# RWKV bonus kept in the mix, a finer planner clock, and another order of the input projections, in a hybrid recurrent layer

## The chip, the cores and the metric

The kernel runs on one core of one Trainium2 chip. The metric is the device time of one execution in microseconds; the median of three runs before is 1594.51 us (1593.97 to 1595.9).

## The reference

One inference step of one layer, all in float32: a prompt of 1024 tokens with zero states, and 8 sample tokens with states of their own (1032 columns together), model width 1024.

```
xn = rmsnorm(x);  P = xn @ w_in            # 1024 x 3456 columns
pr, ph, pl = split(P)                      # RWKV-7 (6 heads), HGRN2 (6 heads), RG-LRU (256 channels)
# A) RWKV-7: pm = pr + mu * (shift(pr) - pr); r, k, v, lora inputs; per token and head
S = S * w_t + (S @ -kk_t) (kk_t * a_t)^T + v_t k_t^T ;   out_t = S r_t
gn    = groupnorm(out) * ln_w + ln_b
bonus = (sum(r * k * r_k) * v)             # per head
o_r   = (gn + bonus) * g
# B) HGRN2: S = f_t * S + (1 - f_t) i_t^T ; o_t = S^T q_t ; rmsnorm per head, silu gate
# C) RG-LRU: conv of width 4, two gates, h_t = a_t h_{t-1} + sqrt(1 - a_t^2) (i_t x_t), gelu gate
mix = concat(o_r, o_h, o_l)                # 384 + 384 + 256
x = x + mix @ w_out
x = x + square(relu(rmsnorm(x) @ mlp_w1)) @ mlp_w2      # 1024 -> 4096 -> 1024
y = rmsnorm(x)
```

Returned are y for both groups and the five final states of each.

## The kernel before

Activations lie transposed, features on the partitions: mix is eight tiles of 128 features, three for RWKV (a pair of heads each), three for HGRN, two for LRU. Time is cut into two halves: half 0 is tokens 0 to 511, half 1 tokens 512 to 1023 with the 8 samples (520 columns). A dense product is done in three reduced-precision (fp32r) matmuls for each block of 128 features: weights and activations are split into a high and a low part (wh, wl, xh, xl, for the output projection mh, ml), and wh x xh, wh x xl, wl x xh are summed. A weight tile is loaded raw on SP's queue (one buffer), ACT copies out wh (L280), and wl comes in one of two ways: for the names in SOON by a subtraction on DVE (L282), for all others by a negative copy on ACT (L284) and a load on POOL's queue that adds the weights to it (L285). wh and wl have two buffers each.

The first part of the program (to 868 us of the profile) is the mixing: norm, input projections, the three recurrences, the output projection. The second is the MLP, which the diff does not touch.

In the first part a planner sets the order of PE's instructions while the program is built. `weave` takes seven streams and a filler, each a generator. A stream issues a few instructions and then yields: a number D holds it for so many us of the planner's own clock `now`; a key holds it until another stream has set that event. `now` goes on by an estimated cost with each matmul (`mm`) and transpose (`tr`). Whenever no stream is due, the filler `projections()` issues two matmuls: the projections of half 0 in ORDER[0], of half 1 in ORDER[1], then `out_proj(0)`, `out_proj(1)` and the first MLP tiles. In ORDER, w is the RWKV lora columns, r0 to r2, h0 to h2, l0 and l1 the projections of one RWKV, HGRN or LRU tile. The order of the other engines' instructions is left to a tile scheduler, with priorities by stream.

RWKV's work is cut into twelve parts q (tile, half, quarter of 256 tokens). A part goes through `rw_operands` (events A, A2; transposes bt and kt, bonus), `rw_inverse` (sc, W and Y levels; event B), `rw_chain` (four chunks of three steps: the products with az, yz and bt, L714, L718, L727; then the outputs; event C) and `rw_finish` (group norm with gsq and gs, transposes oT; event N; then the gate; event P). In before, the bonus stands in a tile "bo" with two buffers, made in `rw_operands` and read in `rw_finish`; the operands of part q wait for event P of part q-2 ahead of it.

HGRN's `hg_half` builds a chunk's attention in levels: kq (DVE L963, ACT, POOL), rq (DVE L971), and the products gram0 to gram7 on PE. `lru` does the convolution, then four gate products lg and the rest of the recurrence on DVE and ACT.

Projected tiles have counted buffers. RWKV's have RPM = 6, and HGRN's and LRU's share HPM = 8: an h item takes four, an l item three, and the filler stops at `take` until a buffer is given back, which `hg_run` and `lru` do at their ends.

The root of half 0's norm is kept in a tile of mix that is written last: in the code it is the tile of the last item of ORDER[0].

In names such as `in2944_1_0`, the numbers are the column of w_in, the half, and the first token column; `out5_0` is row block 5 of the output projection from token column 0; `ch_2_1_1` is the chain of tile 2, half 1, second quarter.

Of the kernel before, what the change touches and what calls it, by code (L numbers as in the profile page):

```python
# [10 lines left out]
F32R = mybir.dt.float32r  # L11
# [6 lines left out]
P = 128  # L18
# [7 lines left out]
HT = 512  # L26
HW = HT + NB
QT = 256
# [12 lines left out]
SOON = tuple(f"in{col}_0" for col in (1152, 1280, 0, 384, 768, 2944, 3200, 1408, 1792, 2176, 2560)) + \  # L41
    ("out0_0", "out1_0") + tuple(f"out{m}_1" for m in range(8)) + tuple(f"w1_{f}" for f in range(4))
PRI = [-100, 0, 0, 300, 300, 300, 100, 300]
ORDER = [[(x[0], int(x[1])) for x in half.split()] for half in ("r0 w0 l0 h0 r1 l1 h1 r2 h2", "w0 r0 h0 r1 h1 l0 r2 h2 l1")]
NFB = FF // (FB * P)

COL_R, COL_K, COL_V, COL_WA, COL_G = 0, 384, 768, 1152, 1280
# [5 lines left out]
def kernel(ctx: ExitStack, tc: tile.TileContext, i, o):  # L53
# [15 lines left out]
    now = [0.0]  # L69
    done = {}  # L70

    def mm(out, lhsT, rhs, start=True, stop=True):
        n, m = rhs.free_size(), lhsT.free_size()
        now[0] += n / 2400 if rhs.dtype == F32R else 0.19 if n < 16 else max(n, m) / (600 if m > 64 else 800)
        PE.matmul(out, lhsT, rhs, start=start, stop=stop)  # L75

    def tr(out, in_, idn):
        now[0] += 0.11
        PE.transpose(out, in_, idn)

    o_busy = [0.0]

    def bank_o(name):

        while now[0] < o_busy[0]:
            yield o_busy[0] - now[0]
        return ps("o", name)

    def used_o(delay=L_O):
        o_busy[0] = now[0] + delay  # L90

    def ev(key, delay=1.5):
        done[key] = now[0] + delay
# [51 lines left out]
    mix = [mixp.tile([P, TP], F32, name=f"mix{k}") for k in range(KT)]  # L145
# [39 lines left out]
    def vec(name, k, n=1):  # L185
        return vt[:, at[name] + k:at[name] + k + n]
# [66 lines left out]
    def head_inv_root(sq, n, name, floor, tmp):  # L253

        pc = yield from bank_o(f"pc_{name}")
        nt = n // P
        for t in range(nt):
            mm(pc[:, 2 * t:2 * t + 2], sq[:, t * P:(t + 1) * P], bones2)
        used_o()
        a = small.tile([P, 2 * nt], F32, tag="ir_kk", name=f"ir_{name}", bufs=1)  # L260
        V.tensor_scalar(a, pc[:, :2 * nt], floor, None, op0=ALU.max)
        rpow(a)

        V.tensor_copy(tmp.rearrange("p (x c) -> p x c", c=64), bc(a[:, :, None], [P, 2 * nt, 64]))
        yield D1
        pb = yield from bank_o(f"pb_{name}")
        for t in range(nt):
            tr(pb[:, t * P:(t + 1) * P], tmp[:, t * P:(t + 1) * P], ident)
        used_o()
        return pb[:, 0:n]  # L270
# [135 lines left out]

    rb0 = mix[dict(r=0, h=3, l=6)[ORDER[0][-1][0]] + ORDER[0][-1][1]][:, 0:HT]
    early = {}
# [93 lines left out]
    def w2(tag, n, bufs=2, name=None):  # L502
        return rwp.tile([P, QT], F32, tag=tag, name=f"{name or tag}_{n}", bufs=bufs)
# [7 lines left out]
    def twice(ap):  # L511

        return bc(ap.rearrange("p (c t) -> p c t", t=C)[:, :, None, :], [P, ap.shape[1] // C, 2, C])

    def rw_operands(q):

        j, hf, qt = PARTS[q]
        n = f"{j}_{hf}_{qt}"
        q0 = qt * QT
        qs = slice(q0, q0 + QT)  # L520
        jc = slice(j * P, (j + 1) * P)
        yield ("lora", hf)
        yield ("rkv", j, hf)
        xwa, _ = lora[hf]
        r, k, v = rkv[j, hf]

        def ck(ap):
            return ap.rearrange("p (c t) -> p c t", t=C)

        def heads_of(out, pt):  # L530

            for h, b in enumerate(brow):
                S.copy(out[b], pt[b].rearrange("p (c h x) -> p c h x", h=2, x=C)[:, :, h])

        r_, k_, v_ = r[:, qs], k[:, qs], v[:, qs]
        t1, t2, t3, t4 = (w2(f"t{u}", n, 1) for u in range(1, 5))

        act(t2, k_, AF.Square, scale=vec("kk", j))

        pw = yield from bank_o(f"pw_{n}")  # L540
        mm(pw[:, 0:QT], wup[:, jc], xwa[:, qs])
        used_o()
        act(t1, pw[:, 0:QT], AF.Tanh, bias=hw0[:, j:j + 1], scale=0.5)
        V.tensor_scalar(t1, t1, -DECAY, -DECAY, op0=ALU.mult, op1=ALU.add)
        yield D4
        pn = yield from head_inv_root(t2, QT, f"kk{n}", 1e-24, t4)
        V.scalar_tensor_tensor(t4, k_, vec("kk", j), pn, op0=ALU.mult, op1=ALU.mult)
        V.tensor_tensor_scan(t2, rmask_f, t1, 0.0, op0=ALU.mult, op1=ALU.add)
        yield D5
        pa = yield from bank_o(f"pa_{n}")  # L550
        mm(pa[:, 0:QT], aup[:, jc], xwa[:, qs])
        used_o()
        act(t3, pa[:, 0:QT], AF.Tanh, bias=ha0[:, j:j + 1], scale=0.5)
        if q >= 3:
            yield ("C", q - 3)
        if q >= 1:
            yield ("sc", q - 1)
        yield D6
        ee = rwp.tile([P, NQ, C + 1], F32, tag="ee", name=f"ee_{n}", bufs=1)
        wc = rwp.tile([P, NQ], F32, tag="wc", name=f"wc_{n}", bufs=3)  # L560
        ar = rwp.tile([P, NQ, 2, C], F32, tag="ar", name=f"ar_{n}", bufs=3)
        bt = rwp.tile([P, NQ, P], F32, tag="bt", name=f"bt_{n}", bufs=3)
        kt = rwp.tile([P, NQ, C], F32, tag="kt", name=f"kt_{n}", bufs=1)
        vr = rwp.tile([P, NQ, C], F32, tag="vr", name=f"vr_{n}", bufs=3)
        G.memset(ee[:, :, 0:1], 1.0)
        act(ee[:, :, 1:C + 1], ck(t2), AF.Exp)
        act(t1, t2, AF.Exp, scale=-1.0)
        V.tensor_copy(wc, ee[:, :, C])

        pt = yield from bank_o(f"vT_{n}")  # L570
        S.copy(bt.rearrange("p c (h t) -> p c h t", t=C), twice(v_))
        for c in range(NQ):
            tr(pt[:, c * P:(c + 1) * P], bt[:, c], ident)
        used_o()
        heads_of(vr, pt)
        V.scalar_tensor_tensor(t2, t3, 1.0, t4, op0=ALU.add, op1=ALU.mult)
        for h, b in enumerate(brow):
            V.scalar_tensor_tensor(kz[b, 0, :, h], ck(t2[b]), 0.5, ck(t1[b]), op0=ALU.mult, op1=ALU.mult)
        V.tensor_scalar(t3, t3, hka[:, j:j + 1], omka[:, j:j + 1], op0=ALU.mult, op1=ALU.add)
        V.tensor_tensor(t3, t3, k_, op=ALU.mult)  # L580
        for h, b in enumerate(brow):
            V.tensor_tensor(kz[b, 1, :, h], ck(t3[b]), ck(t1[b]), op=ALU.mult)
        V.scalar_tensor_tensor(ar[:, :, 0, :], ck(t4), -1.0, ee[:, :, 0:C], op0=ALU.mult, op1=ALU.mult)
        V.tensor_tensor(ar[:, :, 1, :], ck(r_), ee[:, :, 1:C + 1], op=ALU.mult)
        ev(("A", q), L_OPS)
        V.scalar_tensor_tensor(t2, r_, vec("rk", j), t3, op0=ALU.mult, op1=ALU.mult)
        yield D7

        pt = yield from bank_o(f"bt_{n}")
        for c in range(NQ):  # L590
            tr(pt[:, c * P:(c + 1) * P], kz[:, 0, c].rearrange("p h t -> p (h t)"), ident)
        used_o()
        S.copy(bt, pt.rearrange("p (c x) -> p c x", x=P))
        yield D4
        pt = yield from bank_o(f"kt_{n}")
        for c in range(NQ):
            tr(pt[:, c * P:(c + 1) * P], kz[:, 1, c].rearrange("p h t -> p (h t)"), ident)
        used_o()
        heads_of(kt, pt)
        if q >= 2:  # L600
            yield ("P", q - 2)
        yield D8
        bo = w2("bo", n)
        pb = (yield from bank_o(f"bonus_{n}"))[:, 0:QT]
        mm(pb, bones, t2)
        used_o()
        V.tensor_tensor(bo, pb, v_, op=ALU.mult)
        if qt == 1:
            free["pm"] += 3
        live[q] = dict(wc=wc, ar=ar, bt=bt, kt=kt, vr=vr, bo=bo)  # L610
        ev(("A2", q), L_EV)
        yield D9
# [706 lines left out]
    def cols(group, j):  # L1319

        return [c + j * P for c in dict(w=(COL_WA, COL_G), r=(COL_R, COL_K, COL_V), h=(COL_HF, COL_HQ, COL_HI, COL_HG),
                                        l=(COL_LX, COL_LG))[group]]

    def projections():
        for col, bank in zip((col for group, j in ORDER[0] for col in cols(group, j)), ("big", "big", "o")):
            ws_[0] = next_w()
            early[0, col] = yield from project(0, col, 0, HT, bank)
        for hf in range(2):
            for group, j in ORDER[hf]:
                yield from dict(w=rw_lora, r=rw_proj, h=hg_proj, l=lru_proj)[group](j, hf)  # L1330
# [34 lines left out]
    def start():  # L1365

        ahead.extend((lambda col=col, hf=hf: load_w(i["w_in"][col // P], f"in{col}_{hf}", parts=2 if not hf and col == COL_WA else 1))
                     for hf in range(2) for group, j in ORDER[hf] for col in cols(group, j))
        ahead.extend((lambda m=m, hf=hf: load_w(i["w_out"][m], f"out{m}_{hf}")) for hf in range(2) for m in range(KT))
# [226 lines left out]
```

## Time and profile before

| what | before |
|---|---|
| median of 3 runs | 1594.51 us (1593.97 to 1595.9) |
| profiled execution | 1596.51 us, span 1594.7 us |
| PE busy | 1504.8 us, 94% |
| DVE, ACT, POOL busy | 48%, 42%, 24% |
| mean granted clock of PE | 0.972 |

The page gives shares over the whole span. The slices of a fortieth (about 40 us) show where an engine or PE's clock falls off; the view by stages gives busy time, granted clock and DMA share between chosen times; the chain follows the work that ended last back through what released it; the waits name what PE waited for. PEclk is the granted clock of PE, 1.00 being full speed. A row of the timeline is a group of equal instructions with its start, the duration of one and, in brackets, the idle time before it with what ended it.

### The profile page before, as it was taken

The numbers are of one execution on the slowest core, as the hardware profiler recorded it, in microseconds if no ns is written. First come the engines' busy times: TensorE is split into PE (matmuls) and PEld (weight loads), VectorE is DVE, ScalarE is ACT, GpSimd is POOL, SyncE is SP. The second block draws the span as 40 slices with busy tenths as digits, with TensorE's granted clock in tenths as the row PEclk, the third lists the DMA queues.
The fourth block names the chain that finished last, engine by engine and source line by source line (L and its number), as shares of the span: only waits on it lengthen the run. The fifth ranks groups of instructions, "written<-read, shape, count | busy, mean of one in ns | idle before, by whom it ended". The sixth has DMA issues, their size and how long they took to land.

```text
span 1594.7 us, 30262 instructions
## 1 busy us (share of the span) xinstructions
PE 1504.8 (94%) x12536; PEld 1324.2 (83%) x12536; DVE 769.9 (48%) x1799; ACT 663.4 (42%) x1435; POOL 381.5 (24%) x531
## 2 busy tenths in 40 slices
PE   8979998999999988899798999999999999999997
PEld 6757777898888877777697989899999998989887
DVE  7777676666655865764465322222222222222224
ACT  3544745655464562553244424233232423233232
POOL 4553322333334343223222010101111010111011
PEclk9989999999999998899899999999999999999999
DMA  4324442443433432226133443545454454444242
GB/s 164 125 55 105 97 92 68 106 93 70 106 68 95 102 80 74 56 68 153 34 120 93 106 93 80 106 80 106 80 106 80 101 98 91 95 91 95 54 92 107
DMA packets 53081, 146.89 MB, mean 92 GB/s; under 512 B 6960, under 2 KB 7248, under 8 KB 52944
## 3 DMA queue, kind: packets, MB, share of 16 engines
q0 software_dynamic: 22976, 65.33, 24.8%
q1 hardware_dynamic: 29824, 79.61, 15.4%
q8 instruction: 98, 1.61, 0.4%
q14 instruction: 39, 0.32, 0.1%
q10 hardware_dynamic: 144, 0.04, 0.0%
HBM read 138.87 MB, written 6.07 MB: 91 GB/s over the span
## 4 chain that ended last, share of the span: by engine, by line
PE 72%; DVE 8%; DMA 6%; ACT 6%; issue 5%; POOL 3%; SPq 0%; POOLq 0%; ACTq 0%; DVEq 0%
PE up L75 22%; PE dn L75 20%; PE in L75 13%; PE ch L75 3%; PE out L75 3%; PE W L75 2%; PE Y L75 2%; DMA wl_in<-in_w_in 1%; DMA raw_in<-in_w_in 1%; PE gram L75 1%; PE sc L75 1%; DMA raw_out<-in_w_out 1%; DMA raw_w<-in_w 1%; POOL mix L363 1%; ACT wh_in L280 1%
## 5 line engine op out<-in xcount | busy, mean ns | idle before, releaser
L75 PE MATMUL in<-xh,wl_in 128*128 128x512 f32 (+3 forms) x648 | 221.6, 342 | 5.2 <-DMA wl_in<-in_w_in 3.8
L75 PE MATMUL in<-xl,wh_in 128*128 128x512 f32 (+3 forms) x648 | 221.9, 342 | 3.2 <-DVE xl L374 3.2
L75 PE MATMUL dn<-hh,wl_w 128*128 128x264 f32 (+2 forms) x696 | 222.9, 320 | 0.3 <-DMA wl_w<-in_w 0.3
L75 PE MATMUL dn<-hl,wh_w 128*128 128x264 f32 (+2 forms) x696 | 222.8, 320 | 0.0
L75 PE MATMUL in<-xh,wh_in 128*128 128x512 f32 (+3 forms) x648 | 222.3, 343 | 0.5 <-ACT praw_wa L421 0.5
L75 PE MATMUL dn<-hh,wh_w 128*128 128x264 f32 (+2 forms) x696 | 222.6, 320 | 0.0
L1484 DVE TENSOR_TENSOR mix<-mix,dn 128x512 f32<-128x512 f32 (+2 forms) x192 | 98.4, 512 | 241.9 <-PE dn L75 241.9
L285 POOL DMA_DIRECT2D wl_w<-in_w x86 | 76.0, 887 | 573.3 <-ACT hh L1414 305.8
L280 ACT ACTIVATE wh_w<-raw_w 128x512 fp32r<-128x512 f32 (+1 forms) x90 | 70.6, 785 | 283.6 <-PE dn L75 227.4
L1413 DVE SCALAR_TENSOR_TENSOR rl<-up,rl 128x512 f32<-128x512 f32 (+2 forms) x96 | 49.6, 516 | 205.3 <-ACT rl L1412 205.2
L75 PE MATMUL up<-nxh,wh_w 128*128 128x264 f32 (+1 forms) x512 | 145.6, 284 | 0.0
L75 PE MATMUL up<-nxl,wh_w 128*128 128x264 f32 (+1 forms) x512 | 144.8, 283 | 0.4 <-POOL nxl L1310 0.4
L75 PE MATMUL up<-nxh,wl_w 128*128 128x264 f32 (+1 forms) x512 | 145.0, 283 | 0.0
L75 PEld LDWEIGHTS dn<-hh,wl_w 128*128 128x128 f32 x696 | 130.8, 188 | 13.1 <-DMA wl_w<-in_w 2.8
L75 PEld LDWEIGHTS in<-xh,wl_in 128*128 128x128 f32 x648 | 126.4, 195 | 16.8 <-DMA wl_in<-in_w_in 4.8
L75 PEld LDWEIGHTS in<-xl,wh_in 128*128 128x128 f32 x648 | 126.6, 195 | 16.4 <-DVE xl L374 6.6
L75 PEld LDWEIGHTS dn<-hl,wh_w 128*128 128x128 f32 x696 | 130.9, 188 | 10.1
L75 PEld LDWEIGHTS dn<-hh,wh_w 128*128 128x128 f32 x696 | 131.0, 188 | 9.4
L75 PEld LDWEIGHTS in<-xh,wh_in 128*128 128x128 f32 x648 | 126.4, 195 | 11.3 <-issue 1.2
L75 PE MATMUL up<-nh,wh_w 128*128 128x512 f32 x256 | 101.7, 397 | 0.0
L75 PE MATMUL up<-nh,wl_w 128*128 128x512 f32 x256 | 101.5, 396 | 0.0
L75 PE MATMUL up<-nl,wh_w 128*128 128x512 f32 x256 | 101.4, 396 | 0.0
(459 smaller groups left out, 3285.1 us busy)
## 6 DMA issues: line engine op xcount, KB each, us to landing
raw_in<-in_w_in SPq DMA_DIRECT2D x53, 512.0 KB, 3.3
wl_in<-in_w_in POOLq DMA_DIRECT2D x43, 512.0 KB, 5.6
raw_w<-in_w SPq DMA_DIRECT2D x32, 512.0 KB, 3.3
raw_w<-in_w SPq DMA_DIRECT2D x64, 256.0 KB, 2.6
wl_w<-in_w POOLq DMA_DIRECT2D x58, 256.0 KB, 4.1
wl_w<-in_w POOLq DMA_DIRECT2D x28, 512.0 KB, 5.5
raw_out<-in_w_out SPq DMA_DIRECT2D x16, 512.0 KB, 3.3
out_y_prompt<-yt SPq DMA_DIRECT2D x16, 256.0 KB, 2.0
```

The lines of the kernel that those rows point to most:

```text
L75: PE.matmul(out, lhsT, rhs, start=start, stop=stop)
L280: act(wh[:, ks], raw[:, ks], AF.Copy)
L285: G.dma_start(wl[:, ks], src[:, ks], accum_op=ALU.add)
L363: G.tensor_tensor(x, x, rs, op=ALU.mult)
L1413: V.scalar_tensor_tensor(rl[:, :n], pt[:, :n], 0.0, rl[:, :n], op0=ALU.max, op1=ALU.mult)
L1484: V.tensor_tensor(x2[m][:, c0:c0 + n], x2[m][:, c0:c0 + n], pt[:, :n], op=ALU.add)
```

## The change

Three things are edited. The bonus is written into the columns of mix that belong to its own part, instead of the tile "bo", and the wait of a part's operands for the finish of the part two before it is dropped. The planner's costs are others: fp32r matmuls n/2200 for n/2400, small ones by two other formulas, and 0.12 for each change of the shape of the stationary operand (`reshape`). And ORDER is another for each half.

```diff
-ORDER = [... ("r0 w0 l0 h0 r1 l1 h1 r2 h2", "w0 r0 h0 r1 h1 l0 r2 h2 l1")]
+ORDER = [... ("r0 w0 h0 r1 l0 h1 r2 h2 l1", "w0 r0 r1 h0 h1 r2 h2 l0 l1")]
...
     def mm(out, lhsT, rhs, start=True, stop=True):
         n, m = rhs.free_size(), lhsT.free_size()
-        now[0] += n / 2400 if rhs.dtype == F32R else 0.19 if n < 16 else max(n, m) / (600 if m > 64 else 800)
+        reshape(lhsT.shape[0], m)
+        now[0] += n / 2200 if rhs.dtype == F32R else max(n, 112) / 580 if m > 64 else max(n, 36) / 1000
         PE.matmul(out, lhsT, rhs, start=start, stop=stop)
 
     def tr(out, in_, idn):
+        reshape(P, P)
         now[0] += 0.11
         PE.transpose(out, in_, idn)
+
+    shape = [None]
+
+    def reshape(k, m):
+        new = tuple(32 if x <= 32 else 64 if x <= 64 else P for x in (k, m))
+        if new != shape[0]:
+            now[0] += 0.12
+            shape[0] = new
...
         heads_of(kt, pt)
-        if q >= 2:
-            yield ("P", q - 2)
         yield D8
-        bo = w2("bo", n)
+        bo = mix[j][:, hf * HT + q0:hf * HT + q0 + QT]
         pb = (yield from bank_o(f"bonus_{n}"))[:, 0:QT]
         mm(pb, bones, t2)
```

What it does to PE's order is seen at three places. The first is the end of the last RWKV part, ch_2_1_1. In before its chunk steps stand one behind the other after the last matmul of out1 that can be done, and the transposes oT, the gate and the norm's product nc follow its outputs directly:

```order
L75 MATMUL out1_768_9157<-mh7_9043,wl_out1_1_9066 128x264
L75 MATMUL ch_2_1_1_9125<-mv_2_1_1_8608,bt_2_1_1_8179 128x64
L75 MATMUL ch_2_1_1_9125<-st0_2_1_1_9182,az_186 128x64
L75 MATMUL ch_2_1_1_9125<-rh1_2_1_1_9188,yz_187 128x64
L75 MATMUL ch_2_1_1_9125<-mv_2_1_1_8608,bt_2_1_1_8179 128x64
L75 MATMUL ch_2_1_1_9125<-st1_2_1_1_9193,az_186 128x64
L75 MATMUL ch_2_1_1_9125<-rh2_2_1_1_9199,yz_187 128x64
...
L75 MATMUL ch_2_1_1_9125<-vr_2_1_1_8181,sr_2_1_1_8604 64x64
L79 MATMUL oT_2_1_1_9263<-ident_79,ot_2_1_1_9243 128x128 x4
L75 MATMUL gate_2_1_1_9270<-pm_xg1_3261,gup_162 128x256
L75 MATMUL nc_0_9295<-ones_92,acc0_7896 128x1 x4
L75 MATMUL out0_512_9072<-mh2_9038,wh_out0_1_8916 128x256
```

In the changed kernel, on PE too, the same transposes and the same gate stand among the matmuls of the output projection of half 0:

```order
L76 MATMUL out2_0_8872<-mh1_8569,wl_out2_0_8793 128x512
L81 MATMUL oT_2_1_1_8899<-ident_79,ot_2_1_1_8776 128x128 x4
L76 MATMUL out2_0_8872<-mh3_8571,wh_out2_0_8792 128x512
L76 MATMUL out2_0_8872<-ml3_8579,wh_out2_0_8792 128x512
L76 MATMUL out2_0_8872<-mh3_8571,wl_out2_0_8793 128x512
L76 MATMUL out2_0_8872<-mh4_8572,wh_out2_0_8792 128x512
L76 MATMUL out2_0_8872<-ml4_8580,wh_out2_0_8792 128x512
L76 MATMUL out2_0_8872<-mh4_8572,wl_out2_0_8793 128x512
L76 MATMUL out2_0_8872<-mh6_8574,wh_out2_0_8792 128x512
L76 MATMUL out2_0_8872<-ml6_8582,wh_out2_0_8792 128x512
L76 MATMUL gate_2_1_1_8914<-pm_xg1_3756,gup_162 128x256
```

The last part has moved ahead of most of out_proj(0). Between its last output product and oT stand 30 matmuls of out1_0 and out2_0, two other products and one group of transposes.

The second place is PE at the gram levels of the last HGRN item, h2 of half 1. In before output matmuls stand between two levels:

```order
L75 MATMUL gram2_2_1_8031<-rq0_196,kq2_2_1_7961 64x2x32 x8
L75 MATMUL out0_0_7927<-mh6_7903,wh_out0_0_7799 128x512
L75 MATMUL out0_0_7927<-ml6_7911,wh_out0_0_7799 128x512
L75 MATMUL out0_0_7927<-mh6_7903,wl_out0_0_7800 128x512
L75 MATMUL out0_0_7927<-mh7_7904,wh_out0_0_7799 128x512
L75 MATMUL ch_1_1_1_7765<-st1_1_1_1_7998,az_186 128x64
L75 MATMUL out0_0_7927<-ml7_7912,wh_out0_0_7799 128x512
L75 MATMUL out0_0_7927<-mh7_7904,wl_out0_0_7800 128x512
```

In the changed kernel PE's rows there are these (lg are the gate products of the first LRU item, in3072 is the second LRU item's projection):

```order
L76 MATMUL lg0_0_1_0_8303<-lxc0_1_8204,lruw_204 128x260
L76 MATMUL gram2_2_1_8313<-rq0_196,kq2_2_1_8238 64x2x32 x8
L76 MATMUL lg0_0_1_260_8323<-lxc0_1_8204,lruw_204 128x260
L76 MATMUL ch_2_1_1_8330<-st2_0_183,az_186 128x64
L76 MATMUL lg0_1_1_0_8334<-lxc0_1_8204,lruw_204 128x260
L76 MATMUL gram3_2_1_8344<-rq1_197,kq3_2_1_8306 64x2x32 x8
L76 MATMUL ch_2_1_1_8330<-rh0_2_1_1_8332,yz_187 128x64
L76 MATMUL lg0_1_1_260_8356<-lxc0_1_8204,lruw_204 128x260
L76 MATMUL ch_2_1_1_8330<-mv_2_1_1_7640,bt_2_1_1_7413 128x64
L81 MATMUL oT_2_1_0_8365<-ident_79,ot_2_1_0_8284 128x128 x4
L76 MATMUL in3072_1_0_8397<-xh0_3424,wh_in3072_1_8010 128x256
```

No projection matmul stands between the levels now; the filler is held at its buffers, and goes on with in3072. The levels gram0 and gram1 and the end of the chain ch_2_1_0 stand ahead of these rows, behind in3200_1_256, in the same way; a hold of the same kind lies between in2816_1_256 and in2944_1_0.

The third place is PE between two tiles of out_proj(0). In before:

```order
L75 MATMUL out4_0_8663<-mh5_7902,wh_out4_0_8557 128x512
L75 MATMUL hso2_8720<-hq2_1_7093,hsst2_8643 64x1 x16
L75 MATMUL ch_2_1_0_8597<-rh1_2_1_0_8712,yz_187 128x64
L75 MATMUL Y1_2_1_1_8742<-ym_2_1_1_8606,wm1_2_1_1_8691 64x64 x8
L75 MATMUL out4_0_8663<-ml5_7910,wh_out4_0_8557 128x512
L75 MATMUL out4_0_8663<-mh5_7902,wl_out4_0_8558 128x512
L75 MATMUL hsq2_8755<-hssq2_8738,bones_84 128x8
L75 MATMUL out5_0_8775<-mh0_7897,wh_out5_0_8655 128x512
```

and in the changed kernel:

```order
L76 MATMUL out4_0_9027<-mh5_8573,wh_out4_0_8981 128x512
L76 MATMUL out4_0_9027<-ml5_8581,wh_out4_0_8981 128x512
L76 MATMUL out4_0_9027<-mh5_8573,wl_out4_0_8982 128x512
L76 MATMUL out5_0_9065<-mh0_8568,wh_out5_0_9019 128x512
L76 MATMUL out5_0_9065<-ml0_8576,wh_out5_0_9019 128x512
L76 MATMUL out5_0_9065<-mh0_8568,wl_out5_0_9020 128x512
```

The recurrences' products are gone from between the tiles out3_0 to out7_0, whose matmuls follow each other directly.

More of the change, by code (lines that the diff above doesn't have):

```diff
@@ L43 @@
 PRI = [-100, 0, 0, 300, 300, 300, 100, 300]
-ORDER = [[(x[0], int(x[1])) for x in half.split()] for half in ("r0 w0 l0 h0 r1 l1 h1 r2 h2", "w0 r0 h0 r1 h1 l0 r2 h2 l1")]
+ORDER = [[(x[0], int(x[1])) for x in half.split()] for half in ("r0 w0 h0 r1 l0 h1 r2 h2 l1", "w0 r0 r1 h0 h1 r2 h2 l0 l1")]
 NFB = FF // (FB * P)
```

## The prediction

> **What bounds the kernel now.** I read the page first (busy shares and the slices), then the times of each engine by stage, then the chain that ended last and PE's own rows in the stage that stands out, and last the waits on PE.
>
> ```profile
> PE 1504.8 (94%) x12536; PEld 1324.2 (83%) x12536; DVE 769.9 (48%) x1799; ACT 663.4 (42%) x1435; POOL 381.5 (24%) x531
> ...
> PE   8979998999999988899798999999999999999997
> ...
> PEclk9989999999999998899899999999999999999999
> ```
>
> PE is the bound: 94% busy, the next engine at 48%. The diff changes no arithmetic, so only PE's idle time and the stretches in which its clock is below full can change. They lie in the first 22 slices. By stage (columns: from and to, us, then busy time and instructions of PE, PEld, DVE, ACT and POOL, the granted clock, the DMA share, GB/s):
>
> ```profile
> 114.00:585.00 471.00, 444.82 (x5186) 387.77 (x5185) 313.18 (x840) 261.79 (x657) 153.89 (x226) 0.98 0.40 89
> 585.00:687.00 102.00, 86.80 (x868) 77.24 (x868) 66.65 (x172) 45.32 (x102) 32.20 (x43) 0.90 0.30 71
> ...
> 773.00:796.00 23.00, 13.21 (x94) 10.77 (x92) 6.16 (x22) 3.44 (x17) 3.57 (x8) 0.71 0.01 2
> 796.00:868.00 72.00, 65.33 (x457) 61.73 (x458) 45.99 (x87) 30.68 (x59) 19.27 (x22) 0.93 0.33 103
> 868.00:1530.00 662.00, 661.71 (x4205) 597.09 (x4205) 181.70 (x353) 210.29 (x356) 76.54 (x87) 1.00 0.46 92
> ```
>
> The MLP (868 to 1530) is full at clock 1.00 and is not touched. The hole is 773 to 796: 94 matmuls in 23 us at clock 0.71. The chain says what runs there (start us, us, what):
>
> ```profile
> 757.87 1.66 PE ch L75 x46
> ...
> 783.00 3.11 PE ch L75 x48
> ...
> 787.47 0.45 ACT gsq L758 x2
> ...
> 789.63 1.05 POOL gs L141
> ...
> 791.11 1.26 PE oT L79 x4
> ...
> 793.52 1.21 PE gate L75 x2
> ...
> 796.69 2.55 PE out L75 x10
> ```
>
> It is the last RWKV part alone: its four chunk steps, its 48 products, the group norm on ACT and POOL, the transposes (oT), the gate, and only then the output projection's last two k. PE has nothing beside it. Its rows there, and one of the same pair elsewhere:
>
> ```profile
> 692.82 0.33 PE L75 MATMUL ch<-mv,bt 128*128 128x64 f32 x2
> ...
> 775.09 0.43 PE L75 MATMUL ch<-st,az 128*128 128x64 f32 x2 [0.38 <-DVE st L727]
> ...
> 779.86 0.69 PE L75 MATMUL ch<-st,az 128*128 128x64 f32 x2 [0.45 <-DVE st L727]
> ```
>
> Four to five us after dense work ends, a pair takes 0.69 instead of 0.43 us: the clock has halved, with no gap above 0.45 us. So sparse work costs PE twice, by the gaps and by the clock. The waits on PE in the whole span (us in total, times, longest):
>
> ```profile
> PE pb_kk L79 <- DVE t L264: 8.9, 5, 4.2
> PE ch L75 <- DVE st L727: 7.6, 15, 1.2
> PE ch L75 <- DVE rh L714: 6.9, 8, 2.8
> ...
> PE in L75 <- DMA wl_in<-in_w_in: 3.8, 4, 1.7
> ...
> PE s_mean L75 <- DVE s_os L858: 2.8, 1, 2.8
> ```
>
> **The bonus and the missing wait.** The bonus product goes into the columns of mix that its own part will finish, and the operands of part q no longer wait for part q-2 to finish. No instruction is added: the DVE multiply has another target, and before it only PE's product stands. By itself this is worth nothing where PE has other work. What it buys is the end: the parts may run ahead, and in the new PE order the last part's transposes and gate stand among the matmuls of out1_0 and out2_0, with 30 output matmuls between its last product and its transposes, instead of after the whole of out_proj(0). The hole from 774.5 (the end of the last output matmul) to the 796.69 of the chain is 22.2 us. PE's own work in it at full clock: ten pairs of 0.33, 48 products at the 1.66 per 46 of 757.87, half of the 1.26 and the 1.21 (they ran at half clock) and about 0.9 for the norm's eight small products, 3.3 + 1.7 + 1.3 + 0.9 = 7.2. So 15.0 go, and half of the 2.55 of the ten matmuls that ran slowly behind it: **-16**. Bounds: -19 (nothing slow is left in 796 to 868 either, whose clock is 0.93) and -10 (half the steps wait among the output matmuls as the 15 chain steps above do). What is late next is the second half of the output projection, whose k 2 and 5 now find their input ready; 796 to 868 else stays.
>
> **The order of projections.** HGRN's parts come earlier in half 0, and in half 1 both LRU parts come last, behind r2 and h2. A projection may start only when its buffers are free: there are 8 of a kind, of which HGRN part takes 4 and LRU part 3. Behind h1 and h2 (8) the first LRU part must wait for h1's end, and behind h2 and l0 (7) the second for l0's. In the new PE order no projection matmul stands in two places: 57 rows between in2816_1_256 and in2944_1_0 (hold A), and the part between in3200_1_256 and in3072_1_0 (hold B). Before, output or input matmuls stood in between everywhere.
>
> ```profile
> L963 DVE TENSOR_TENSOR kq<-b x34: 679/685/805, 122.8 to 680.8; 128x512 f32<-128x512 f32 x34
> L964 ACT ACTIVATE kq<-kq x34: 397/417/441, 123.5 to 681.6; 128x256 f32<-128x256 f32 x34
> ...
> L971 DVE TENSOR_TENSOR rq<-kq,hq x68: 377/422/942, 124.3 to 683.1; 64x256 f32<-64x256 f32 x68
> ...
> 679.10 0.57 PE L75 MATMUL W<-xm,sa 64*64 64x64 f32 x14
> ...
> 680.07 0.69 PE L75 MATMUL gram<-rq,kq 128*64 128x64 f32 x16
> 680.68 0.71 PE L75 MATMUL lg<-lxc,lruw 128*128 128x260 f32 x2
> ...
> 685.57 0.69 PE L75 MATMUL gram<-rq,kq 128*64 128x64 f32 x16
> ```
>
> Hold B holds gram0 to gram3, four lg, seven chain pairs, the 48 products of a part's end and four transposes: 4 x 0.69 + 4 x about 0.5 (0.71 is one with its tail) + 7 x 0.33 + 1.7 + 0.6, some 9 us. A gram level follows the last by 5.5 us (680.07 to 685.57) where PE is shared; alone it needs kq 0.69, its exponential 0.42, two rq of 0.42 and its products 0.69, 2.6 us. Four levels are 10.5 to 22 us, so PE idles 1 to 13 us. I take 5, nearer the lower end, since nothing else delays DVE and ACT there, and add 1 for the clock, half of a stretch of two us. Hold A carries some 15 us of PE work of three streams (nine W and Y groups at 0.57 to 0.69, five groups of four transposes or products at about 0.6, six chain pairs, a part's 48 products, the HGRN output), which interleave, so 0 to +8: I take 2. Together **+8**, from +1 to +22. The half 0 order moves only what is beside a full PE: nothing, with the last item's name (mix5 becomes mix7 for the first root) without a wait.
>
> [...]
>
> **Output projection, half 0.** It is now what fills beside the last part, and it outlasts it: out3_0 to out7_0 run as 24 matmuls in a row with nothing between, where before chain and gram products stood in each tile.
>
> ```profile
> 745.34 1.06 ACT L280 ACTIVATE wh_out<-raw_out 128x1024 fp32r<-128x1024 f32 x1 [4.09 <-PE out L75]
> 746.84 1.04 ACT L284 ACTIVATE wl_out<-wh_out 128x1024 fp32r<-128x1024 f32 x1
> ...
> 748.57 0.90 POOL L285 DMA_DIRECT2D wl_out<-in_w_out  x1 [0.15 <-issue]
> ...
> wl_out<-in_w_out POOLq DMA_DIRECT2D x2, 512.0 KB, 5.5
> ...
> 749.17 0.40 PE L75 MATMUL out<-mh,wl_out 128*128 128x512 f32 x1
> 749.40 0.39 PE L75 MATMUL out<-mh,wh_out 128*128 128x512 f32 x1
> ```
>
> A matmul follows the last by 0.23 us, so a tile takes 24 x 0.23 = 5.5 us. The weights of tile m+1 go into the buffers of tile m-1. From there: 745.34 to 748.57 + 5.5 = 754.1, 8.7 us. Tile m covers 5.5 and the first two matmuls 0.5, so 2.7 us are open; the tile behind it then has its weights in time. Two such tiles are **+5**; 0 if the copies are issued early enough (8.0 in the shortest such path, and ACT and POOL are less busy there), +10 if every tile waits. [...]
>
> **The truer clock.** The planner now counts more for a projection matmul (n/2200 for n/2400: its 0.213 us for 512 columns become 0.233, which is the 0.23 of the rows above) and for small ones. A step held for so many us by the plan thus has some 7 to 9% less PE work behind it. Steps with slack do not notice. Without slack is pb_kk, above all the one at the start:
>
> ```profile
> 75.80 12.13 POOL L363 TENSOR_TENSOR mix<-mix,xrb 128x520 f32<-128x520 f32 x8
> ...
> 92.20 1.02 POOL L141 TENSOR_TENSOR ir_kk<-ir_kk,mhalf 128x4 f32<-128x4 f32 x1
> ...
> 99.27 0.41 PE L79 MATMUL pb_kk<-ident,t 128*128 128x128 f32 x2 [4.17 <-DVE t L264]
> ```
>
> POOL's normalisation of half 1 stands before the root that pb_kk needs; it ends no earlier, and PE reaches pb_kk with less behind it: **+2**, from -3 (the projections ahead of it come in another order) to +5. The other eleven parts: 585 to 687 idles 15.2 of 102 us at clock 0.90, against 26.2 of 471 at 0.98 in the stretch before. There parts wait for each other, s_mean and the 2.8 us of rh among them, which the free parts and the pair r0, r1 in a row relieve. At the earlier stretch's rate it would idle 5.7, a gain of 9.5, with 8 for the clock: -17 at best. Twelve shorter distances that each miss by up to 0.7 us are +8. I take **-5**, a third of the best, since the distances alone (the waits on pb_kk, 8.9 us) already have no margin.
>
> **Sum.** -16 + 8 + 5 + 2 - 5 = -6. The profiled execution took 1596.5 us around its span of 1594.7; the median of the runs is 1594.5, 2 less. So the profiled run goes to about 1590.5 and the runs to 1588. A measurement of this kernel can tell about 0.2%, 3.2 us, from no change.
>
> **Rivals.** *The hole moves instead of closing (slower).* The mechanism is the buffer limit in hold A and B. If the four levels keep their 5.5 us pace, B costs 13, A its 8, with some 5 for the half clock of 20 us: +26 where I have +8, so 1606. With the other terms as above it decides from holds of 17 us on (16 - 5 - 2 + 5 = 14 is break-even, and 3.2 more can be told). For it: PE has no filler there at all, as in 773 to 796. Against: three streams share the holds, not one.
>
> *The gain is given back (same).* Holds +10, the weights' path +8, and -2 instead of -5: -16 + 10 + 8 + 2 - 2 = +2, 1596. For it: dense out_proj(0) is new, and the accumulating load is the slowest step in it. That the missing wait changes nothing ends here too: if the parts do not finish sooner on the chip, only the -16 shrinks to -10.
>
> *More goes (faster still).* The 585 to 687 stalls go by -14 and the holds cost 4: -16 + 4 + 4 + 2 - 12 = -18, 1577. For it: the clock of 0.90 is a consequence of the same stalls. Against: the tighter distances.
>
> **How the numbers follow.** My forecast, 1581 to 1591: 0.55. More goes, 1572 to 1581: 0.10. Same, 1591.3 to 1597.7: 0.17. Slower, 1598 to 1608: 0.18. So faster 0.65, same 0.17, slower 0.18. The range leaves some two in ten outside, the lower end of the third rival and the upper part of the first: 1574 to 1602.
>
> **What would show it.** Right: no stretch like 773 to 796 is left; gsq, gs, oT and gate of the last part stand beside output matmuls at clock 1.00; two stretches of 5 to 20 us without in or out matmuls stand before out_proj(0), with waits on gram from kq or rq; waits of PE's out on the DMA of wl_out (0.3 us before) of 2 to 3 us at two or more tiles; pb_kk waits no less than its 8.9 us. Wrong: the holds run at a clock near 0.7 and add over 17 us; or the idle of 585 to 687 appears in another place of half 1, where r0 and r1 now stand in a row and the HGRN parts follow without a filler between.

## The result, and the profile after

The changed kernel takes 1619.99 us (median of 4 runs, 1614.79 to 1623.88) against 1594.24 us of the kernel before: 26 us more, ratio 1.0162, 95% interval 1.0141 to 1.0184. Its profiled execution took 1622.78 us, span 1621.0. Its page, in the lines that were shown of before:

```profile
PE 1509.3 (93%) x12536; PEld 1328.9 (82%) x12536; DVE 776.3 (48%) x1799; ACT 661.4 (41%) x1435; POOL 382.1 (24%) x531
...
PE   8879898989899898888899999999999999999997
...
PEclk9979999999999999989999999999999999999999
```

PE is busy for as long as before (1509.3 for 1504.8 us); the time is new idle time. The slice of 7 ahead of the MLP is gone, but slices of 8 stand now over the whole first half. For the account the span is cut where the work changes: the first pb_kk (the product that spreads an RWKV part's root over its tile), the first projection of half 1, the first matmul of out_proj(0) and of out_proj(1), the first MLP tile. Before, by stage (columns as in the prediction):

```profile
57.00:293.00 236.00, 217.50 (x2091) 172.34 (x2091) 165.52 (x372) 130.91 (x292) 78.15 (x112) 0.97 0.38 86
293.00:662.00 369.00, 341.40 (x4058) 313.75 (x4057) 232.81 (x653) 190.62 (x487) 129.04 (x181) 0.95 0.38 86
662.00:764.00 102.00, 93.75 (x989) 73.44 (x988) 65.43 (x162) 49.22 (x129) 31.20 (x44) 0.97 0.40 100
764.00:840.00 76.00, 63.97 (x506) 60.47 (x507) 41.33 (x87) 24.82 (x54) 16.64 (x21) 0.89 0.24 78
```

and after:

```profile
57.00:330.00 273.00, 241.52 (x2401) 194.69 (x2402) 186.03 (x429) 134.84 (x324) 85.99 (x125) 0.94 0.33 75
330.00:734.00 404.00, 364.84 (x4439) 331.40 (x4438) 255.40 (x710) 201.83 (x524) 136.77 (x195) 0.95 0.35 79
734.00:808.00 74.00, 63.36 (x403) 49.55 (x402) 36.62 (x79) 36.38 (x78) 23.22 (x27) 0.93 0.54 137
808.00:866.00 58.00, 52.57 (x404) 51.41 (x402) 32.99 (x55) 20.16 (x34) 10.42 (x11) 0.94 0.31 96
```

The lengths cannot be compared, since the streams do other shares of their work in each stage (the counts of matmuls show it). What can is what PE lost in each: its idle time (length less busy) and the length times what the clock lacks to 1.00. The second is an estimate, since it counts the missing clock over idle time too. Worked out so:

| PE's loss, us (idle + clock) | before | after | difference |
|---|---|---|---|
| half 0's projections | 18.5 + 7.1 = 25.6 | 31.5 + 16.4 = 47.9 | +22 |
| half 1's projections | 27.6 + 18.5 = 46.1 | 39.2 + 20.2 = 59.4 | +13 |
| out_proj(0) | 8.3 + 3.1 = 11.4 | 10.6 + 5.2 = 15.8 | +4 |
| out_proj(1) | 12.0 + 8.4 = 20.4 | 5.4 + 3.5 = 8.9 | -11.5 |

The sum is +28 for a span 26.3 longer; the start and the MLP differ by less than 2. So the hole of the last part is closed, and its gain is given back three times over, most of it in half 0, 300 us and more ahead of the places that the change seemed to be about. The waits on PE over the whole span (us in total, times, longest):

```profile
PE pb_kk L81 <- DVE t L275: 16.6, 5, 9.3
PE ch L76 <- DVE st L737: 14.3, 12, 3.4
PE W L76 <- DVE xm L697: 10.4, 10, 2.6
PE ho L76 <- DVE hst L1060: 6.6, 9, 1.7
PE out L76 <- DMA wl_out<-in_w_out: 5.9, 3, 2.3
```

pb_kk, ch, W and out on the DMA were 8.9, 7.6, 1.4 and 0.3. The row of ch is one of three that DVE ends; together they are 17.1 us for 18.7 before, so pb_kk and W grew and the chain did not. The last part's end, PE's rows in the timeline:

```profile
764.40 0.60 PE L81 MATMUL oT<-ident,ot 128*128 128x128 f32 x4
...
766.68 0.59 PE L76 MATMUL gate<-pm_xg,gup 128*128 128x256 f32 x2
```

They wait for nothing and run at a granted clock of 1.00 (0.60 us for the four transposes; 1.25 at 0.50 before), beside the output projection, as forecast. The largest single wait is at the start of half 0. POOL's rows there, then PE's:

```profile
74.00 12.40 POOL L374 TENSOR_TENSOR mix<-mix,xrb 128x520 f32<-128x520 f32 x8 [1.92 <-ACT xrb L371]
...
91.29 1.47 POOL L152 TENSOR_TENSOR ir_kk<-ir_kk,mhalf 128x4 f32<-128x4 f32 x1
```

```profile
81.84 0.61 PE L76 MATMUL pc_kk<-bones,t 128*128 128x2 f32 x4 [2.27 <-ACT t L554]
...
96.67 0.66 PE L81 MATMUL pb_kk<-ident,t 128*128 128x128 f32 x2 [9.31 <-DVE t L275]
```

The sums pc_kk are there at 82.5; the root that POOL makes of them stands behind the normalisation of half 1 and ends at 92.8. That was so before too (the root ran from 92.2 to 93.2), but PE had work until 95.1 there and has it only until 87.4 here. Behind the root stands DVE's copy of it, beside the rest of POOL's normalisation here and behind it before. DVE's row here, then the one before:

```profile
92.79 3.73 DVE L275 COPY t<-ir_kk 128x256 f32<-128x256 f32 x1 [0.49 <-POOL ir_kk L152]
```

```profile
98.83 0.29 DVE L264 COPY t<-ir_kk 128x256 f32<-128x256 f32 x1
```

So 3.7 us of the wait of 9.3 are this copy. The two holds, A and then B, as stages of PE, and PE's longest wait in each:

```profile
637.00:670.00 33.00, 27.62 (x468) 23.92 (x469) 21.32 (x61) 13.56 (x56) 13.01 (x18) 0.91 0.20 52
699.00:718.00 19.00, 14.70 (x166) 11.49 (x166) 15.67 (x39) 12.29 (x38) 7.11 (x10) 0.81 0.27 56
```

```profile
PE hsq L76 <- DVE hssq L1115: 2.1, 1, 2.1
...
PE ch L76 <- DVE st L737: 1.8, 1, 1.8
```

Together they lose 9.7 us of idle time and 6.6 of clock; no gap of PE in them ends with kq or rq, which the prediction named. And out_proj(0)'s dense tiles wait for their weights:

```profile
779.98 0.50 PE L76 MATMUL out<-mh,wl_out 128*128 128x512 f32 x1 [1.95 <-DMA wl_out<-in_w_out]
787.49 0.50 PE L76 MATMUL out<-mh,wl_out 128*128 128x512 f32 x1 [1.68 <-DMA wl_out<-in_w_out]
795.62 0.50 PE L76 MATMUL out<-mh,wl_out 128*128 128x512 f32 x1 [2.30 <-DMA wl_out<-in_w_out]
```

### The profile page after: what moved, and what is told of

It is laid out like the page before. It is cut to its first block, busy times and chain, and to the rows that moved or that the text cites. A ratio compares the mean times of both kernels' runs of the same rounds, so it can differ in the third digit from the quotient of the medians.

```text
span 1621.0 us, 30309 instructions
## 1 busy us (share of the span) xinstructions
PE 1509.3 (93%) x12536; PEld 1328.9 (82%) x12536; DVE 776.3 (48%) x1799; ACT 661.4 (41%) x1435; POOL 382.1 (24%) x531
## 4 chain that ended last, share of the span: by engine, by line
PE 61%; DVE 14%; issue 8%; DMA 6%; ACT 6%; POOL 4%; POOLq 0%; SPq 0%; ACTq 0%; DVEq 0%
PE up L76 20%; PE dn L76 17%; PE in L76 10%; PE ch L76 2%; PE out L76 2%; PE W L76 2%; PE Y L76 1%; DMA raw_out<-in_w_out 1%; DMA wl_in<-in_w_in 1%; DMA raw_w<-in_w 1%; PE sc L76 1%; DMA wl_w<-in_w 1%; POOL mix L374 1%; PE gram L76 1%; ACT gsq L768 1%
```

## The experiments

The change has four parts that can be undone singly: the bonus (with the dropped wait), the planner's costs, the order of half 0, the order of half 1. Each time stands beside the kernel before on the same chip (medians 1591.4 to 1593.8 us). One kernel's runs spread by 2 to 14 us, and the stage losses below come from one profile each (that of after_old_half0 is 6.5 us below its median), so a few us between two stages mean little.

**The bonus alone.** On the kernel before:

```diff
-        if q >= 2:
-            yield ("P", q - 2)
         yield D8
-        bo = w2("bo", n)
+        bo = mix[j][:, hf * HT + q0:hf * HT + q0 + QT]
```

> The kernel before with the bonus in the mix and without the wait for part q-2, old orders, old planner clock. Theory of the prediction: freeing the parts by itself lets the last part finish beside output matmuls, the hole of 22 us goes: about 1578 us. Theory now: in its PE order the gate of the last part still stands behind its transposes with no output matmul between, so the hole stays; the order of half 1 is needed too: 1591 to 1597 us, with a hole at clock 0.7 to 0.8 ahead of out2 of the second half.

1614.59 us, ratio 1.0132 (1.0111 to 1.0153): 22 us more, which neither theory had. The hole stays, as the PE order said: the transposes of the last part still wait, 4.8 us for 5.0. Most of the new loss, 25 of 28 us by the stages, is in half 1's projections.

```profile
PE oT L79 <- DVE ot L761: 4.8, 1, 4.8
```

```profile
295.00:698.00 403.00, 364.33 (x4290) 334.62 (x4289) 248.97 (x690) 197.74 (x519) 136.15 (x190) 0.92 0.35 79
```

38.7 us idle and 32 of clock, 71 in all for 46 before. So the freed parts do not by themselves close the hole (out_proj(1) still loses 14 us, for 20); with the old costs they cost a great deal.

**One part undone at a time.** The changed kernel with one old string of ORDER, or with the old `mm` and `tr`:

```diff
# after_old_half0
-ORDER = [... ("r0 w0 h0 r1 l0 h1 r2 h2 l1", "w0 r0 r1 h0 h1 r2 h2 l0 l1")]
+ORDER = [... ("r0 w0 l0 h0 r1 l1 h1 r2 h2", "w0 r0 r1 h0 h1 r2 h2 l0 l1")]
# after_old_half1
+ORDER = [... ("r0 w0 h0 r1 l0 h1 r2 h2 l1", "w0 r0 h0 r1 h1 l0 r2 h2 l1")]
# after_old_clock
+        now[0] += n / 2400 if rhs.dtype == F32R else 0.19 if n < 16 else max(n, m) / (600 if m > 64 else 800)
```

> The changed kernel with the old order of half 0 alone. At equal PE work the changed kernel is some 30 us behind when half 0 ends. Theory H0 (HGRN's first part sooner crowds DVE and POOL beside the second norm and the first RWKV part): it comes back to 1590 to 1597 us. Rival C (the new planner costs put too little work between steps, wherever they stand): it stays at 1613 to 1622 us. Rival M (both by halves): 1603 to 1610.

> The changed kernel with the old order of half 1 alone. Holds of the filler go, which cost 15 to 20 us at equal work; but the last part's gate falls back behind out_proj(0) in the PE order, so the hole of some 16 us returns: 1617 to 1624 us if both are so. If the holds are dear and the hole is not reopened: about 1604. If the holds cost nothing: 1636.

> The changed kernel with the old planner costs. Theory H0 (the orders do it): within 6 us of 1620, the hole stays closed. Rival C (the costs do it, by shorter distances): 1590 to 1600 us, and the waits of PE on pb_kk (16.6 us), ch (17 us) and W (10.4 us) fall to those of before (8.9, 18.7, 1.4).

All three come back to the kernel before: 1593.69 us, ratio 1.0003 (0.9985 to 1.0021); 1595.49, 1.0012 (0.9999 to 1.0025); 1594.39, 1.0008 (0.9994 to 1.0023). For half 0 that is what theory H0 said. For the old order of half 1 no theory had it (1604 or more was expected). For the old costs the time is that of rival C, its signs only in part: pb_kk falls to 6.9 us and W to 6.0, but pc_kk waits 10.6 for 3.5. Three parts that each give back 26 cannot add. The stages tell more than the times. Half 0's projections of after_old_half0, then both projection stages of after_old_half1, then those of after_old_clock:

```profile
57.00:303.00 246.00, 225.36 (x2142) 179.77 (x2140) 174.03 (x400) 133.55 (x298) 83.71 (x120) 0.97 0.37 83
```

```profile
57.00:332.00 275.00, 244.86 (x2397) 197.67 (x2396) 185.38 (x429) 135.23 (x324) 86.09 (x125) 0.93 0.33 74
332.00:696.00 364.00, 338.41 (x4136) 310.15 (x4135) 242.09 (x668) 196.38 (x494) 131.11 (x181) 0.98 0.38 87
```

```profile
57.00:322.00 265.00, 237.62 (x2391) 190.94 (x2390) 191.53 (x435) 133.81 (x312) 86.59 (x125) 0.95 0.34 77
322.00:717.00 395.00, 363.68 (x4438) 331.15 (x4438) 253.24 (x711) 203.94 (x537) 137.23 (x195) 0.94 0.35 80
```

Half 0 loses 28 us with its old order, 49 and 41 with the new one. Half 1's projections lose 33 with their old order, 26 less than in after: the holds are 12 of them (nine_buffers, below), the rest is open. The hole that comes back costs some 6. With the old costs they lose 55. The old costs also leave half 0 some 7 cheaper and the end of out_proj(1) 5; where the rest of their 26 comes from, the stages don't say. Undoing half 0's order also takes 12 us from half 1's projections, which lose 48 there.

**The order of half 0 alone,** on the kernel before:

> The kernel before with the new order of half 0 alone. In the traces so far PE's idle and half-clock time between the first pb_kk and the end of half 0's projections is 41 to 51 us in the three kernels with the new order of half 0 and 25 to 29 in the three with the old. Theory H0 (this order costs that by itself): 1607 to 1613 us. Rival (only together with the bonus or the new clock): 1590 to 1597 us.

1608.22 us, ratio 1.0096 (1.0072 to 1.0121), as theory H0 said. Its stage, and its longest waits on PE, both at 75 to 105 us:

```profile
57.00:305.00 248.00, 220.33 (x2131) 175.91 (x2130) 171.62 (x375) 126.10 (x283) 80.07 (x114) 0.94 0.36 82
```

```profile
PE pc_kk L75 <- ACT t L543: 11.4, 3, 9.4
...
PE pb_kk L79 <- DVE t L264: 6.2, 2, 5.2
```

42.6 us lost for 25.6, with 12 of the 17 in the first 73 us. This order costs by itself. The 9.4 us are seen further back: ACT's t stands behind an instruction that waits 9.2 us for DVE's scan b, and DVE's row for two such scans, beside POOL's normalisation of half 1, is

```profile
77.62 10.79 DVE L949 TENSOR_TENSOR_SCAN b<-rmask,lf 128x256 f32<-128x256 f32 x2 [2.00 <-ACT lf L924]
```

The first of them takes 10.2 us; the median of the kernel's twelve is 0.69, and the same row was 3.42 in before. after_old_clock, with the same order of half 0 and the same old costs, has the same longest wait on pc_kk, 9.4 us.

**The two causes taken away, and a control.** In no_half1_norm 15 POOL instructions are left out, in nine_buffers there is one buffer more and an LRU item takes its buffers when it needs them:

```diff
# no_half1_norm, in norm1
-            G.tensor_tensor(x, x, rs, op=ALU.mult)
-            G.tensor_scalar(x, x, vec("g1", k), 0.0, op0=ALU.mult, op1=ALU.add)
+            if k == 0:
+                G.tensor_tensor(x, x, rs, op=ALU.mult)
# nine_buffers
-RPM, HPM = 6, 8
+RPM, HPM = 6, 9
...
-        for w in ("xb", "gl", "gq"):
-            yield from take("hpm")
-            x.append(hp_tile(f"l{w}{t}_{hf}"))
+        yield from take("hpm")
+        xb = hp_tile(f"lxb{t}_{hf}")
...
+        for w in ("gl", "gq"):
+            yield from take("hpm")
+            x.append(hp_tile(f"l{w}{t}_{hf}"))
```

> The changed kernel with 15 of the 16 POOL instructions left out that normalise half 1's activations (75 to 95 us of its trace); the planner does not see them, so PE's order stays. Theory P (the 9.3 us wait of pb_kk, and the 13.7 us at half clock around it, are POOL's queue ahead of the root): that wait falls below 3 us and the time by 8 to 12, 1608 to 1612 us. Rival (DVE is late there anyway, its copy from the root takes 3.7 us): the wait stays above 6 us, 1616 to 1622.

> The changed kernel with nine instead of eight HGRN and LRU buffers, of which an LRU item takes one for its first projection and two more only for its second. In PE's order no stretch without projection matmuls longer than 36 rows is left in half 1. Theory B (the two holds cost 10 to 15 us of idle and half clock): 1605 to 1611 us. Rival (three streams fill the holds, what is missing there was only moved): 1616 to 1622.

> The changed kernel with nine buffers taken singly and without the 15 POOL instructions that normalise half 1. If the two causes are separate: 1620 - 12 - 12, 1593 to 1599 us, about the kernel before. If they are one (the late half 0 makes the holds dear): 1604 to 1609 us, no better than either alone.

> The kernel before without the same 15 POOL instructions. Its pb_kk waits 4.2 us there and an lg 3.3 us, with half clock in three windows. If the early hole is the change's own: 1588 to 1594 us, 0 to 5 less. If the kernel before pays the same: 1579 to 1584 us, 10 to 14 less, and the 12 us in the changed kernel explain nothing of the difference.

Without the normalisation 1608.2 us, ratio to before 1.0086 (1.0061 to 1.011); with nine buffers 1607.58, 1.0087 (1.0064 to 1.011); with both 1596.42, 1.0024 (1.001 to 1.0039). So each is worth 12 us in the changed kernel, and they add: two separate causes. The holds' share is the change's own: with both old orders nine buffers gain nothing (1584.87 us for 1583.24, table below). It is not 12 everywhere: with the old order of half 0 alone they gain 7 (1586.62 for 1593.69). The first is not the change's own: before_no_norm takes 1583.97, 0.9933 (0.991 to 0.9956), so the kernel before pays 10 us for the same normalisation. The first 73 us of the stage, of before, before_no_norm, after and no_half1_norm:

```profile
57.00:130.00 73.00, 63.08 (x450) 49.12 (x450) 55.64 (x97) 34.95 (x60) 31.02 (x40) 0.93 0.29 73
```

```profile
57.00:130.00 73.00, 69.80 (x585) 54.86 (x585) 54.96 (x110) 40.04 (x71) 16.95 (x23) 0.98 0.36 88
```

```profile
57.00:130.00 73.00, 60.30 (x482) 49.16 (x482) 54.67 (x94) 29.16 (x55) 34.10 (x44) 0.88 0.27 66
```

```profile
57.00:130.00 73.00, 71.17 (x661) 57.36 (x661) 54.03 (x117) 34.60 (x68) 21.41 (x29) 0.95 0.29 74
```

The early hole loses 15.0 us before and 21.5 after, and 4.7 and 5.5 without POOL's work: 10 and 16. The change adds 2 us by the times and 6 by the stages to a hole that was there. What the left-out work did is two things that these runs do not separate: it stood ahead of the root on POOL, and DVE was slower beside it. Without it DVE's copy of the root takes 0.30 us for 3.73, and no scan b more than 0.75 us. The rest of half 0's +22 lies behind 130 us: PE loses 25 us there for 10 before, but 15 with the new order on the kernel before (half0_alone) and 13 in after_old_clock. So most of this part needs the new order and the new costs together; by which step is open.

**Which move in half 0.** In the changed kernel, one of the two moves undone:

```diff
# old_l0_new_l1
-"r0 w0 h0 r1 l0 h1 r2 h2 l1"
+"r0 w0 l0 h0 r1 h1 r2 h2 l1"
# new_l0_old_l1
+"r0 w0 h0 l0 r1 l1 h1 r2 h2"
```

> The changed kernel with the first LRU item of half 0 back ahead of HGRN's first (r0 w0 l0 h0 r1 h1 r2 h2 l1). Theory (HGRN's level work ahead of the first RWKV part's DVE, ACT and POOL steps is what costs): 1592 to 1602 us. Rival (the late second LRU item, which leaves half 1's start to fewer streams): 1612 to 1622.

> The changed kernel with HGRN's first item still first, and the second LRU item back at its old place (r0 w0 h0 l0 r1 l1 h1 r2 h2). Theory (HGRN sooner costs): 1610 to 1622 us. Rival (the late LRU item costs): 1592 to 1602.

1607.9 us, ratio 1.0105 (1.0075 to 1.0136), and 1608.89, 1.0109 (1.0085 to 1.0133): each undoes half, and neither theory holds alone. The projection stages of the first, then of the second:

```profile
57.00:320.00 263.00, 240.65 (x2459) 193.25 (x2458) 187.63 (x441) 137.49 (x329) 87.85 (x125) 0.97 0.34 77
320.00:721.00 401.00, 367.21 (x4371) 335.68 (x4370) 250.74 (x694) 200.62 (x521) 133.85 (x192) 0.92 0.35 79
```

```profile
57.00:310.00 253.00, 226.82 (x2127) 181.46 (x2126) 172.94 (x391) 134.85 (x299) 82.40 (x116) 0.93 0.35 80
310.00:725.00 415.00, 381.22 (x4705) 347.16 (x4705) 263.61 (x746) 202.83 (x549) 139.75 (x202) 0.94 0.33 77
```

Half 0 itself loses 30 us with LRU's first item ahead, about as little as with the old order (28), and 44 with HGRN's ahead: HGRN sooner, or, which is the same move, LRU later, is what costs there. The late second LRU item costs 12 us by the time. With LRU's first item ahead the stages put it into half 1's projections, which lose 66 for 48 with the whole old order of half 0; with HGRN's ahead they show it nowhere in particular, and why it costs is open.

**The costs, and better versions.**

> The changed kernel with both old orders: the bonus in the mix and the new planner costs. If the parts add (half 0 as before, half 1's input stage as in after_old_half1, where idle and half clock are 34 us for 45 before, the hole of the last part still there): 1576 to 1584 us. Rival (the kernels' gains do not add, each order meets its own stalls): 1590 to 1597. If the bonus alone is what costs (it cost 22 us with the old clock): over 1605.

> The kernel before with the new planner costs alone. With the bonus in the mix and old orders the new costs gain 31 us (bonus_alone 1614.6, bonus_and_clock 1583.2). Theory G (the costs are better wherever they stand): below 1585 us. Theory R (they only repair what the freed parts break with the old costs, the parts held by their waits cannot use them): 1590 to 1598 us. If longer than 1600: they cost where the parts are held.

> The changed kernel with the old order of half 0 and nine buffers taken singly: both things that cost most are undone, the hole stays closed. If the gains add (after_old_half0 1593.7, nine buffers 12 less): 1578 to 1585 us. Rival (the holds were dear only behind the late half 0): 1590 to 1596.

> bonus_and_clock with nine buffers taken singly: old orders, so the last part still ends alone. Theory (no hold to fill, since the old order of half 1 has none): 1580 to 1587 us, as bonus_and_clock, with the hole at half clock ahead of the second half of the output projection. Rival (earlier LRU projections help by themselves): 1572 to 1578.

> As nine_old_orders, but in half 1 the two LRU items last (w0 r0 h0 r1 h1 r2 h2 l0 l1): RWKV and HGRN items alternate as in the old order, and in PE's order 40 output matmuls stand between the last part's products and its transposes, 8 between these and the gate. Theory (closing the hole is worth 8 to 12 us, as the stages of after against before show): 1572 to 1577 us. Rival (what the hole gives is taken by the h2 and LRU recurrences that now end later): 1582 to 1590.

| run | bonus | costs | order 0 | order 1 | buffers | us | ratio to before |
|---|---|---|---|---|---|---|---|
| clock_alone | old | new | old | old | 8 | 1596.21 | 1.0018 (1.0003 to 1.0033) |
| bonus_alone | new | old | old | old | 8 | 1614.59 | 1.0132 (1.0111 to 1.0153) |
| bonus_and_clock | new | new | old | old | 8 | 1583.24 | 0.9942 (0.9916 to 0.9968) |
| nine_old_half0 | new | new | old | new | 9 | 1586.62 | 0.996 (0.994 to 0.9981) |
| nine_old_orders | new | new | old | old | 9 | 1584.87 | 0.9945 (0.992 to 0.9969) |
| nine_lru_last | new | new | old | LRU last | 9 | 1581.11 | 0.9924 (0.9895 to 0.9954) |

The new costs gain nothing alone (theory R) and are worth 31 us with the free parts. bonus_and_clock and nine_old_orders came where their theories had them; nine_old_half0 and nine_lru_last fell between theory and rival. Half 1's projections lose 39 us in bonus_and_clock, 46 before:

```profile
57.00:300.00 243.00, 220.29 (x2142) 175.50 (x2142) 174.35 (x400) 133.53 (x298) 84.21 (x120) 0.99 0.37 84
300.00:676.00 376.00, 348.03 (x4324) 318.65 (x4324) 250.29 (x693) 197.81 (x519) 136.62 (x186) 0.97 0.37 84
676.00:760.00 84.00, 76.95 (x711) 60.80 (x710) 46.69 (x112) 40.60 (x94) 24.53 (x37) 0.96 0.48 121
760.00:827.00 67.00, 58.42 (x465) 56.64 (x464) 37.70 (x67) 23.04 (x50) 13.75 (x15) 0.90 0.27 88
```

The last row still has the hole (clock 0.90). nine_lru_last closes it; its row there and its wait for weights:

```profile
773.00:827.00 54.00, 49.21 (x404) 48.22 (x403) 32.99 (x56) 20.07 (x34) 10.43 (x11) 1.00 0.33 104
```

```profile
PE out L76 <- DMA wl_out<-in_w_out: 6.3, 3, 3.0
```

It is the fastest measured, 12.7 us below the kernel before and 38.9 below the changed one; against the other three with the free parts and the new costs the intervals overlap. The hole's 10 us do not show in full: out_proj(0) runs dense instead and waits 6.3 us for its weights.

## Why the prediction was wrong

It forecast 1588 us, range 1574 to 1602, faster with 0.65; the changed kernel takes 1620.

*The step that failed is the order of half 0,* "moves only what is beside a full PE: nothing". I looked at the holds of half 1 and never priced half 0's order. PE lost 25.6 us in that stage before, so it was not full, and it lost 47.9 after. The order alone costs 15 us, and undoing it in the changed kernel gives 26. Of the mechanism the rows show the early part: DVE's scans and copies beside POOL's normalisation, and a root that PE reaches with less work left. Behind 130 us it is known only that most of the loss needs the new costs too.

*The wait of pb_kk,* +2: it grew by 5.1 us, to 9.3, where the upper end of my range was +5. That POOL's normalisation holds the root is shown (without it the long wait is gone); the part that is new is 2 to 6 us. That DVE's copy of the root would take 3.7 us beside POOL, and not 0.3, was in no term.

*The hole,* -16: the mechanism was right, the size a little too large (20.4 to 8.9, -11.5), and its cause was put in the wrong place. Freeing the parts does not close it (bonus_alone); with free parts, the old order of half 1 leaves it (bonus_and_clock), the new one closes it. No run had the new order of half 1 without the bonus.

*The holds,* +8: 12 by nine_buffers, within +1 to +22, under-sized mostly in the clock (6.6 us of it where I had 1). The waits on gram that should have shown them did not come: the longest end with hssq and st. The rival "the hole moves instead of closing" named this place; its +26 was too much for it, and it was not what made the kernel slower alone.

*The weights of out_proj(0),* +5: three waits, 5.9 us, right. The loads took 6.4 us there, where the term reckoned with the 5.5 of before.

*The costs and the free parts elsewhere,* -5: right in sign only with the old orders, where both together gain 10 us. With the new orders the old costs are 26 us better, with the old orders 31 worse, so no sign of theirs holds in general, and a sum of parts, each priced with the others as in before, could not have come out. That should have been in the width of the range.

What stays open: why the free parts cost 22 us with the old costs, and why the new costs are expensive with the new orders (beyond the holds, some 12 us of it lie in half 0 behind 130 us).

## What to carry to other kernels

Where a planner writes one engine's order, an edit of the order is priced in every stage that has idle time, the first one too; a stage in which the bound engine is 92% busy is not "full". Parts of such a change are tried singly and in pairs: here all four together cost 26 us and two of them gain 10. Before a stream is filled up to its buffers, look at who can then be held: one buffer more, and taking each at its first use instead of in a lump, gave 12 us here, 7 beside another order and nothing where no hold was. And a short step that the bound engine waits for is better not left beside a long row of another engine's work; look at its own time there too (DVE's copy of the root took 3.73 us beside POOL's normalisation in after, where the median of its twelve is 0.29).

## What the runs showed of the hardware

In hold B (after, 699 to 718 us) the longest wait of PE is 1.8 us, and the granted clock over its 19 us is 0.81. Two stretches at 0.50 begin in it: from 707.3 us for 3.4 us, with one gap of 1.8 us in the 3.4 us ahead of it, and from 714.1 for 6.8 us, with one gap of 1.45 us in the 3.4 us ahead. In before the clock is 0.50 from 779.3 us for 6.8 us, and the 3.4 us ahead of that hold four gaps of 0.32 to 0.45 us, 1.4 us in all; the 3.4 us before those, with 0.7 us of gaps, are followed by a clock of 1.00. So in these three places a half clock begins behind 1.4 to 1.8 us of idle time in 3.4 us, in one gap or in four. Beside POOL's normalisation one scan of DVE took 10.2 us (half0_alone) and one copy 3.73 (after), for medians of 0.69 and 0.29 of the same kernel's twelve; without the normalisation the copy took 0.30 us and no scan b more than 0.75. And the accumulating 512 KB load took 5.5 us beside the sparse tiles of before (735 to 757 us) and 6.4 where the tiles ran dense (after, 770 to 803 us), on POOL's queue between the loads of x:

```profile
wl_out<-in_w_out POOLq DMA_DIRECT2D x4, 512.0 KB, 6.4
xr<-in_xt POOLq DMA_DIRECT2D x5, 256.0 KB, 6.9
```
